# Turning the softmax reciprocals and the output gate on VectorE instead of TensorE

## The chip, the core and the metric

The kernel runs on one core of a Trainium2 chip. The metric is the device time of one execution in microseconds. Runs of the kernel before took 562.09 us as a median of three (561.46 to 562.93). A profile of one further execution stands beside them; its numbers are used below. TensorE is called PE in the rows, VectorE DVE, ScalarE ACT, GpSimd POOL, and SyncE, which issues most DMAs, SP.

## The reference

One encoder layer on 512 rows (8 by 64 tokens) of 1024 columns. All is float32.

```python
mod = silu(c) @ w_c + b_c                      # 3072 numbers
shift, scl, gate = split(mod, 3)
h = rms_norm(x, g_pre) * (1 + scl) + shift
xa, za, q, k, v, zb, ga, gb = split(h @ w_in, 8)
y_a = (rg_lru(conv(xa), forward) + rg_lru(conv(xa), backward)) * silu(za)
y_b = neighbourhood_attention(q, k, v, rpb) * silu(zb)   # 16 heads of 64; softmax over 8 x 16 neighbours
merged = sigmoid(ga) * (y_a @ w_pa) + sigmoid(gb) * (y_b @ w_pb)
out = rms_norm(x + gate * (merged @ w_o), g_final)
```

## The kernel before

Every product is taken in three passes of a one-pass float format: each float32 operand is split into a high and a low part (ACT casts the high part, DVE or POOL subtracts it), and `mm3` (L386) adds high x high, high x low and low x high in PSUM. `h` is kept with its 1024 columns on partitions as eight tiles of 128 x 512, and `proj` (L689) makes one tile of 128 columns of a projection from one 512 KB tile of weights: load, cast, subtraction, 24 matmuls.

The stages follow one another: start-up (`c`, norm, `h`) together with the projection for v to 60 us; attention, four groups of two pairs of heads, to about 262 us; the recurrent branch with the projection of y_b; the merge (`merge`, L1129) to about 490 us; and the output product with residual and final norm (`epi`, L1169).

The order of all instructions is written by a planner (`Plan`, L99). Each piece of work is an `op` with an engine, a cost, a rank, and the tiles that it reads and writes; the planner steps through its own time, and on each engine takes the piece with the lowest rank among those that can begin soonest. Tiles of 128 x 512 come from 36 slots (`T`), tiles of 128 x 1024 from 32 (`W`), PSUM from 8 banks with a limit for each class (`LIMITS`, L35). A load with `spare=n` is placed only when n more slots are free. `lock=True` keeps a DVE piece and POOL apart in the plan. `after` ties a piece to the begin of a projection, by its place in the list `main`. Each engine then executes its instructions in the written order, and SP's queue is in order too.

In the attention, `attend` (L797) takes the scores' softmax by blocks: DVE adds the bias and finds the minimum (L821), ACT takes the exponential and its sum into `sm`, TensorE turns the block (L835), ACT and DVE split it (L841, L843), and TensorE multiplies with v (L850). The sums `sm` of one pair of heads are 128 queries x 8 (4 blocks of queries by 2 heads). Their reciprocals are wanted along the free axis, one row for each head, spread over 64 partitions each. For that DVE takes the reciprocal (L877), TensorE turns 128 x 8 to 8 x 128 (L882, PSUM class `mi`), ACT copies it with a factor 0.5 (L883), SP writes it to a scratch in DRAM (L885), and two loads read it back spread over partitions (L888).

In the merge stage `gate_row` (L1084) computes the gate as a row: sixteen loads of 128 x 512 of w_c's last third, each multiplied with a column of silu(c) and added up over DVE (L1095, L1097), the sum over partitions by a matmul with ones in two passes (L1109, class `mi`), the bias added and halved (L1113, L1115). The two halves of the gate scale the rows of `w_o` before these are split (L1155). The shift and scale of the modulation are made otherwise, in the start-up: the transposed tile of w_c times the row of silu(c) (`silr`), summed along the free axis by one DVE instruction (L569).

In `epi` the last tile of rows has its right half in two pieces of 256 columns. For the last piece DVE squares and sums, ACT and DVE take the root and a Newton step, then DVE multiplies the right 512 columns by the row's factor and g_final (L1207) and SP writes them out, while ACT scales the left 512 columns (L1210) and writes them out from its own queue.

Of the kernel before, what the change touches and what calls it, by code (L numbers as in the profile page):

```python
# [331 lines left out]
@with_exitstack  # L332
def layer(ctx, tc, x, x_t, par, w_m, w_g, bc_gate, w_v, w_in, w_blk, rpb, amask, w_pa, w_pb, w_o, g_final, out):
    nc = tc.nc
# [60 lines left out]
    def const(name, shape, dt=F32):  # L395
        return pl.fixed(cp.tile(shape, dt, name=name))

    ident, onesc, onesr = const("ident", [P, P]), const("onesc", [P, P]), const("onesr", [P, P], F32R)
    prm, silc, msk, par_sb = const("prm", [P, 120]), const("silc", [P, KD]), const("msk", [P, 80]), const("par_sb", [120, P])
    tan8 = const("tan8", [8, P])  # L400
# [11 lines left out]
    pp0 = B("mi")  # L412
    op("PE", 0.25, lambda e: nc.tensor.transpose(pp0.ap[:, :120], par_sb.ap, ident.ap[:120, :120]), -20,
       r=[par_sb, ident], w=[pp0])
    op("DVE", 0.3, lambda e: nc.vector.tensor_copy(prm.ap, pp0.ap[:, :120]), -20, r=[pp0], w=[prm])
    pc = lambda a, b: prm.ap[:, a:b]
# [13 lines left out]
    for n in range(2):  # L430
        cb = B("hx")

        def f(e, n=n, cb=cb):
            for k in range(4):
                nc.tensor.matmul(cb.ap[:, k * P:(k + 1) * P], ident.ap[:120, 4 * n + k:4 * n + k + 1].to_broadcast([120, P]), par_sb.ap,
                                 start=True, stop=True)
# [96 lines left out]
    def modulate(k):  # L533

        for m, d in ((1, scs), (0, shs)):
# [4 lines left out]
            if k == 0:  # L540
# [18 lines left out]
                continue  # L559
            load(t, whole(t), w_m[2 * k + m], k - 5, 524288, spare=2, name=f"wc{k}{m}")  # L560
            if k == 1:
# [127 lines left out]
    def proj(w, rh, rl, lo="DVE"):  # L689
# [107 lines left out]
    def attend(pr, sps, z, nbt, pos, pos0):  # L797
# [3 lines left out]
        def half(bs):  # L801
# [70 lines left out]
        nz, oz = z  # L872
        sz, rc, rcb = T("sz"), C("rc", 8), B("mi")
        op("ACT", act(512), lambda e: nc.scalar.activation(sz.ap, oz.ap, AF.Tanh, scale=0.5), nz - 1.9, r=[oz], w=[sz], name="zt")
        op("DVE", dve(512), lambda e: nc.vector.scalar_tensor_tensor(sz.ap, sz.ap, 1.0, oz.ap, op0=ALU.add, op1=ALU.mult),
           nz - 1.9, r=[oz], rw=[sz], name="sz")
        op("DVE", 0.17, lambda e: nc.vector.reciprocal(rc.ap, sm.ap), pos - 0.3, r=[sm], w=[rc], name="rc")  # L877


        rct, rcx = T("rct"), T("rcx")  # L880
        scr = pl.fixed(dp.tile([8, P], F32, name=f"rscr{pr}"))
        op("PE", 0.15, lambda e: nc.tensor.transpose(rcb.ap[:8, :P], rc.ap, ident.ap), pos - 0.3, r=[rc, ident], w=[rcb], name="rcb")  # L882
        op("ACT", 0.3, lambda e: nc.scalar.activation(rct.ap[:8, :P], rcb.ap[:8, :P], AF.Copy, scale=0.5), pos - 0.3, r=[rcb], w=[rct],  # L883
           name="rct")
        op("SP", 0.5, lambda e: nc.sync.dma_start(scr.ap, rct.ap[:8, :P]), pos - 3, r=[rct], w=[scr], size=4096, late=SLACK, name="rcs")  # L885
        for h in range(2):
# [11 lines left out]
    def small(rank, after):  # L898
# [3 lines left out]
        op("ACT", 0.22, lambda e: nc.scalar.activation(lt[1].ap, lt[0].ap, AF.Exp, scale=-1.0), rank, r=[lt[0]], w=[lt[1]])  # L902
        op("DVE", 0.2, lambda e: nc.vector.tensor_scalar(silc.ap, pc(0, 8), 0.5, None, op0=ALU.mult), rank, r=[prm], w=[silc])

# [179 lines left out]
    def gate_row(pos, after):  # L1084
        op("ACT", 0.3, lambda e: nc.scalar.copy(onesr.ap, onesc.ap), pos, r=[onesc], w=[onesr], after=after)
        g = (T("g"), T("g"))
        for kk in range(KD):
            for n in range(2):
                wr = T("wr")
                load(wr, whole(wr), w_g[kk * P:(kk + 1) * P, n * 512:(n + 1) * 512], pos + 0.5 * kk, 262144,  # L1090
                     after=after, spare=12, name="wr")

                def f(e, kk=kk, n=n, wr=wr):
                    if kk == 0:
                        nc.vector.tensor_scalar(g[n].ap, wr.ap, silc.ap[:, 0:1], None, op0=ALU.mult)  # L1095
                    else:
                        nc.vector.scalar_tensor_tensor(g[n].ap, wr.ap, silc.ap[:, kk:kk + 1], g[n].ap, op0=ALU.mult, op1=ALU.add)  # L1097
                op("DVE", dve(512), f, pos + 3 + 0.5 * kk, r=[wr, silc], **({"rw": [g[n]]} if kk else {"w": [g[n]]}), lock=True,
                   name="grow")
        for n in range(2):  # L1100
            gh, gl = T("gh", F32R), T("gl", F32R)
            op("ACT", act(512), cast(whole(gh), whole(g[n])), pos + 8, r=[g[n]], w=[gh])
            op("DVE", dve(512), sub(whole(gl), whole(g[n]), whole(gh)), pos + 8, r=[g[n], gh], w=[gl], lock=True)
            o, bcg, gf = B("mi"), T("gate"), T("gfin")

            def f(e, gh=gh, gl=gl, o=o):
                mm(o.ap, onesr.ap, gh.ap, True, False)
                mm(o.ap, onesr.ap, gl.ap, False, True)
            op("PE", 0.46, f, pos + 8, r=[onesr, gh, gl], w=[o], name="grow")  # L1109
            load(bcg, whole(bcg), bc_gate[n * 512:(n + 1) * 512].partition_broadcast(P), pos + 7, 262144, after=after, spare=8)  # L1110

            def f(e, o=o, bcg=bcg):
                nc.vector.tensor_tensor(bcg.ap, o.ap, bcg.ap, op=ALU.add)  # L1113

                nc.vector.tensor_scalar(bcg.ap, bcg.ap, 0.5, None, op0=ALU.mult)  # L1115
            op("DVE", dve(512) + dve2(512), f, pos + 8.2, r=[o], rw=[bcg], lock=True, name="gate")
# [52 lines left out]
    def epi(t, c0, w, o, rank, last):  # L1169
# [150 lines left out]
```

## Time and profile before

| | |
|---|---|
| median of 3 runs | 562.09 us (561.46 to 562.93) |
| the profiled execution | 561.7 us, span 559.8 us |
| TensorE busy | 551.0 us, 98%, granted clock 0.999 |
| DVE, ACT, POOL busy | 391.2, 323.6, 101.9 us |
| chain that ended last | PE 88%, DMA 8%, SP queue 1%, DVE 1% |
| last matmul to the end of the span | 553.4 to 559.8 us |

The span runs from the first to the last instruction; the execution's time has 1.9 us more around it. Matmuls are pipelined: a single one shows its latency, and a piece of the chain of waits shows what a run of them took.

### The profile page before, as it was taken

To read this page: it belongs to the slowest core of one execution; us is meant where nothing else is said; L and a number is where in the kernel's file an instruction comes from. 1 tells how busy PE (TensorE), PEld (TensorE's weight loads), DVE (VectorE), ACT (ScalarE), POOL (GpSimd) and SP (SyncE) were. 2 spreads that over 40 slices of the span, in tenths; PEclk is the share of its full clock that TensorE was granted. 3 is DMA by queue.
4 is the path that set the end of the run, shared out by engine and by line. 5 is a ranking of instruction groups with operands and counts; after the bars stand their busy time and mean duration, and the time that the engine had idled before them with its cause. 6 is when DMAs were issued, how large, how long until landed. Compare 5 with 4: busy or idle time off the path is not lost.

```text
span 559.8 us, 7687 instructions
## 1 busy us (share of the span) xinstructions
PE 551.0 (98%) x2781; PEld 458.6 (82%) x2781; DVE 391.2 (70%) x696; ACT 323.6 (58%) x568; POOL 101.9 (18%) x95
## 2 busy tenths in 40 slices
PE   8999999999999999999999999999999999999995
PEld 8788888788888888887887888888788888888885
DVE  5999733684784876897569648866967897469523
ACT  6542623862763763787965984995698243223243
POOL 1103549555455440000000000000000000000220
PEclk9999999999999999999999999999999999999999
DMA  8993899346437434034332134032319462380002
GB/s 299 408 408 112 305 274 277 139 108 179 120 113 202 113 116 167 2 97 151 112 116 92 39 112 143 28 114 75 114 63 365 136 189 75 130 321 1 0 39 112
DMA packets 35580, 83.47 MB, mean 149 GB/s; under 512 B 3615, under 2 KB 10967, under 8 KB 35543
## 3 DMA queue, kind: packets, MB, share of 16 engines
q1 hardware_dynamic: 35264, 82.66, 44.6%
q8 instruction: 22, 0.36, 0.3%
q10 hardware_dynamic: 279, 0.32, 0.2%
q14 instruction: 15, 0.12, 0.1%
HBM read 76.65 MB, written 6.32 MB: 148 GB/s over the span
## 4 chain that ended last, share of the span: by engine, by line
PE 88%; DMA 8%; SPq 1%; DVE 1%; issue 0%; ACT 0%; POOL 0%; ACTq 0%; POOLq 0%
PE acc L384 72%; PE hx L384 8%; DMA wraw<-in_w_in_dram 3%; DMA vt<-vscr 3%; PE pv L384 3%; PE gt L384 2%; PE pt L835 2%; PE sp L384 2%; DMA wv<-in_w_v_dram 1%; DMA xT<-in_x_t_dram 1%; SPq L373 1%; SPq L678 1%; DVE va L675 0%; POOL vl L381 0%; PE mi L384 0%
## 5 line engine op out<-in xcount | busy, mean ns | idle before, releaser
L384 PE MATMUL acc<-hhl,whi 128*128 128x512 f32 x784 | 244.6, 393 | 0.0
L384 PEld LDWEIGHTS acc<-hhl,whi 128*128 128x128 f32 x784 | 143.9, 188 | 27.7
L384 PE MATMUL acc<-hhl,wlo 128*128 128x512 f32 x392 | 152.9, 390 | 0.0
L384 PEld LDWEIGHTS acc<-hhl,wlo 128*128 128x128 f32 x392 | 73.6, 188 | 15.6
L378 ACT CAST whi<-wraw 128x1024 fp32r<-128x1024 f32 x72 | 74.1, 1043 | 7.3 <-DMA wraw<-in_w_in_dram 6.6
L1186 POOL TENSOR_TENSOR yo<-yo,gfin 128x512 f32<-128x512 f32 x6 | 8.1, 1350 | 337.2 <-ACT xr L1183 337.2
L381 POOL TENSOR_TENSOR wlo<-wraw,whi 128x1024 fp32r<-128x1024 f32 x23 | 56.0, 2441 | 53.8 <-ACT whi L378 41.2
L381 DVE TENSOR_TENSOR wlo<-wraw,whi 128x1024 fp32r<-128x1024 f32 x49 | 59.2, 1220 | 9.3 <-ACT whi L378 9.1
L384 PE MATMUL acc<-woh,mhl 128*128 128x512 f32 (+1 forms) x144 | 40.4, 365 | 0.0
L384 PE MATMUL acc<-ybhl,whi 128*128 128x512 f32 x128 | 39.4, 389 | 0.0
L384 PE MATMUL acc<-yahl,whi 128*128 128x512 f32 x128 | 39.4, 389 | 0.0
L736 POOL TENSOR_TENSOR nb<-msk,braw 128x192 f32<-128x192 f32 (+1 forms) x48 | 30.7, 668 | 43.1 <-DMA braw<-in_rpb_dram 29.6
L828 ACT ACTIVATE p<-p,mn 128x192 f32<-128x192 f32 (+1 forms) x64 | 30.5, 477 | 5.8 <-DVE mn L821 5.7
L384 PE MATMUL hx<-vh,hhl 128*128 128x512 f32 x112 | 33.5, 389 | 0.0
L821 DVE CUSTOM_DVE_ANT_0 p<-sp,nb 128x192 f32<-128x192 f32 (+1 forms) x64 | 31.7, 607 | 0.9 <-PE sp L384 0.7
L1061 DVE SCALAR_TENSOR_TENSOR gm<-gm,acc 128x512 f32<-128x512 f32 x16 | 11.0, 687 | 28.6 <-PE acc L384 28.5
L384 PEld LDWEIGHTS acc<-woh,mhl 128*128 128x128 f32 x144 | 26.1, 189 | 4.4
L843 DVE TENSOR_TENSOR pp<-pt,pp 128x384 fp32r<-128x384 f32 (+1 forms) x32 | 19.8, 625 | 12.7 <-ACT pp L841 12.3
L384 PEld LDWEIGHTS acc<-yahl,whi 128*128 128x128 f32 x128 | 24.0, 188 | 5.0
L384 PEld LDWEIGHTS acc<-ybhl,whi 128*128 128x128 f32 x128 | 24.0, 188 | 5.0
L967 DVE SCALAR_TENSOR_TENSOR xc<-acc,prm,xc 128x511 f32<-128x511 f32 (+1 forms) x24 | 18.0, 749 | 12.3 <-ACT xc L960 11.7
L384 PE MATMUL acc<-wol,mhl 128*128 128x512 f32 (+1 forms) x72 | 26.3, 365 | 0.0
(202 smaller groups left out, 964.4 us busy)
## 6 DMA issues: line engine op xcount, KB each, us to landing
wraw<-in_w_in_dram SPq DMA_DIRECT2D x56, 512.0 KB
wc<-in_w_m_dram SPq DMA_DIRECT2D x14, 512.0 KB
vt<-vscr SPq DMA_DIRECT2D x24, 256.0 KB
vscr<-va SPq DMA_DIRECT2D x8, 512.0 KB
wraw<-in_w_pb_dram SPq DMA_DIRECT2D x8, 512.0 KB
wraw<-in_w_pa_dram SPq DMA_DIRECT2D x8, 512.0 KB
wr<-in_w_g_dram SPq DMA_DIRECT2D x16, 256.0 KB
wo<-in_w_o_dram SPq DMA_DIRECT2D x8, 512.0 KB
```

Of the source, the lines that this page charges most:

```text
L373: return op("SP", 0.45, lambda e: nc.sync.dma_start(dst(), src() if callable(src) else src), rank, r=r, w=[t], after=after, spare=spare, s ...
L378: return lambda e: nc.scalar.copy(o(), i()) if e == "ACT" else nc.vector.tensor_copy(o(), i())
L381: return lambda e: ENGINE[e].tensor_tensor(o(), a(), b().bitcast(F32), op=ALU.subtract)
L384: nc.tensor.matmul(o, a, b, start=first, stop=last)
L736: nc.gpsimd.tensor_tensor(o, mv, view, op=ALU.subtract)
L821: nc.vector.tensor_tensor_reduce(out=o, in0=v(spv(h, e)[:, :nk]), in1=v(nb[:, h, :nk]), scale=1.0, scalar=3e38, op0=ALU.add, op1=ALU.min, ...
L828: nc.scalar.activation(pv2(i), pv2(i), AF.Exp, bias=mn.ap[:, c:c + 1], scale=-1.0, accum_out=sm.ap[:, 2 * b + h:2 * b + h + 1])
L835: nc.tensor.transpose(ptp.ap[:, j * P:(j + 1) * P], pt_.ap[:, j * P:(j + 1) * P], ident.ap)
L843: op("DVE", dve(nt * P), lambda e_, ppv=ppv, pv4=pv4: nc.vector.tensor_tensor(ppv()[:, :, 1, :], pv4(), ppv()[:, :, 0, :].bitcast(F32), op ...
L967: nc.vector.scalar_tensor_tensor(a, b, wcol, a, op0=ALU.mult, op1=ALU.add)
L1061: op("DVE", dve(512), lambda e: nc.vector.scalar_tensor_tensor(t.ap, t.ap, 1.0, o.ap, op0=ALU.add, op1=ALU.mult), n - 1.9, r=[o], rw=[t], ...
L1186: op(("DVE", "POOL"), (dve(w), pool_(w)), lambda e: ENGINE[e].tensor_tensor(y(), y(), gfin[n].ap[:, gs], op=ALU.mult), rank + 0.1, r=[gfin ...
```

## The change

- `attend`: DVE doubles the 128 x 8 sums, takes the reciprocals into the first 8 columns of a fixed 128 x 32 tile (`rc0` or `rc1`, filled with ones once by POOL), and turns that tile in pieces of 32 by 32. SP writes the 128 x 32 result to a scratch of 32 x 128 in DRAM through the view `turned`, which puts piece b of 32 partitions at columns 32b: 128 runs of 32 numbers. The two loads that read rows back stay. The transpose on TensorE and the copy on ACT go.
- The gate is made as a column, like shift and scale: eight loads of 512 KB of the transposed w_c, at ranks 17 to 24, each times `silr` and summed by one DVE instruction, at ranks 20 to 27; then halved, turned in pieces of 32 by 32, and written to a scratch. `gate_row` now only loads the two halves from that scratch, spread over 128 partitions. The sixteen loads, the row's sums, its split and its four matmuls go, with the constants `onesr` and `silc`.
- The parameters' block has 128 rows in place of 120, as it takes in the gate's bias.
- `epi`: in the last tile the piece of columns 512 to 767 is multiplied by g_final as soon as it is squared. At the end DVE multiplies only columns 768 to 1023 by factor and g_final, then scales columns 448 to 767; SP writes columns 448 to 1023, and ACT scales and writes 0 to 447.

```diff
+GR = 17
...
-    op("PE", 0.25, lambda e: nc.tensor.transpose(pp0.ap[:, :120], par_sb.ap, ident.ap[:120, :120]), -20,
+    op("PE", 0.25, lambda e: nc.tensor.transpose(pp0.ap[:, :P], par_sb.ap, ident.ap), -20,
...
+    def turned(scr):
+        return bass.AP(scr.tensor, scr.offset, [[32, 4], [P, 32], [1, 32]])
...
+    rcs = [const(f"rc{i}", [P, 32]) for i in range(2)]
+    for t in rcs:
+        op("POOL", 0.1, lambda e, t=t: nc.gpsimd.memset(t.ap, 1.0), 8, w=[t], after=[main[6]])
...
-        sz, rc, rcb = T("sz"), C("rc", 8), B("mi")
+        sz, rc = T("sz"), rcs[pr % 2]
...
-        op("DVE", 0.17, lambda e: nc.vector.reciprocal(rc.ap, sm.ap), pos - 0.3, r=[sm], w=[rc], name="rc")
+        def recip(e):
+            nc.vector.tensor_scalar(rc.ap[:, :8], sm.ap, 2.0, None, op0=ALU.mult)
+            nc.vector.reciprocal(rc.ap[:, :8], rc.ap[:, :8])
+            nc.vector.transpose(rct.ap[:, :32], rc.ap)
...
-        scr = pl.fixed(dp.tile([8, P], F32, name=f"rscr{pr}"))
-        op("PE", 0.15, lambda e: nc.tensor.transpose(rcb.ap[:8, :P], rc.ap, ident.ap), pos - 0.3, r=[rc, ident], w=[rcb], name="rcb")
-        op("ACT", 0.3, lambda e: nc.scalar.activation(rct.ap[:8, :P], rcb.ap[:8, :P], AF.Copy, scale=0.5), pos - 0.3, r=[rcb], w=[rct],
-           name="rct")
-        op("SP", 0.5, lambda e: nc.sync.dma_start(scr.ap, rct.ap[:8, :P]), pos - 3, r=[rct], w=[scr], size=4096, late=SLACK, name="rcs")
+        scr = pl.fixed(dp.tile([32, P], F32, name=f"rscr{pr}"))
+        op("DVE", 0.5, recip, pos - 0.3, r=[sm], w=[rc, rct], name="rc")
+        op("SP", 0.5, lambda e: nc.sync.dma_start(turned(scr.ap), rct.ap[:, :32]), pos - 3, r=[rct], w=[scr], size=16384, late=SLACK, name="rcs")
...
+    gcol, gtur = const("gcol", [P, 32]), T("gtur")
+    gscr = pl.fixed(dp.tile([32, P], F32, name="gscr"))
+    op("POOL", 0.1, lambda e: nc.gpsimd.memset(gcol.ap, 0.0), 8, w=[gcol])
+    for k in range(KD):
+        t, r = W("wc"), gcol.part()
+        load(t, whole(t), w_m[3 * k + 2], GR + k, 524288, after=[main[GR + k - 2]], spare=6, name=f"wc{k}2")
+        op("DVE", dve(1024) + 0.08, lambda e, k=k, t=t: nc.vector.tensor_tensor_reduce(
+            out=t.ap, in0=t.ap, in1=silr.ap, scale=0.5, scalar=pc(120 + k, 121 + k), op0=ALU.mult, op1=ALU.add,
+            accum_out=gcol.ap[:, k:k + 1]), GR + 3 + k, r=[silr, prm], rw=[t], w=[r], lock=True, name="gate")
+    def turn(e):
+        nc.vector.tensor_scalar(gcol.ap[:, :8], gcol.ap[:, :8], 0.5, None, op0=ALU.mult)
+        nc.vector.transpose(gtur.ap[:, :32], gcol.ap)
+    op("DVE", 0.35, turn, GR + 12, rw=[gcol], w=[gtur], name="gturn")
+    op("SP", 0.5, lambda e: nc.sync.dma_start(turned(gscr.ap), gtur.ap[:, :32]), GR + 12, r=[gtur], w=[gscr], size=16384, late=SLACK, name="gscr")
...
     def gate_row(pos, after):
-        op("ACT", 0.3, lambda e: nc.scalar.copy(onesr.ap, onesc.ap), pos, r=[onesc], w=[onesr], after=after)
-        g = (T("g"), T("g"))
-        for kk in range(KD):
-            for n in range(2):
-                wr = T("wr")
-                load(wr, whole(wr), w_g[kk * P:(kk + 1) * P, n * 512:(n + 1) * 512], pos + 0.5 * kk, 262144,
-                     after=after, spare=12, name="wr")
...
         for n in range(2):
...
-            op("PE", 0.46, f, pos + 8, r=[onesr, gh, gl], w=[o], name="grow")
-            load(bcg, whole(bcg), bc_gate[n * 512:(n + 1) * 512].partition_broadcast(P), pos + 7, 262144, after=after, spare=8)
...
+            bcg, gf = T("gate"), T("gfin")
+            load(bcg, whole(bcg), bass.AP(gscr.ap.tensor, gscr.ap.offset + n * 512, [[0, P], [1, 512]]), pos + 7, 262144, r=[gscr],
+                 after=after, spare=8)
...
-            if t < NT - 1 or n == 0:
+            if t < NT - 1 or c0 + w < D:
                 op(("DVE", "POOL"), (dve(w), pool_(w)), lambda e: ENGINE[e].tensor_tensor(y(), y(), gfin[n].ap[:, gs], op=ALU.mult),
...
-            z, zz = (lambda: yo[t].ap[:, 512:]), (lambda: yo[t].ap[:, :512])
-            op("DVE", dve(512), lambda e: nc.vector.scalar_tensor_tensor(z(), z(), rs.ap, gfin[1].ap, op0=ALU.mult, op1=ALU.mult),
-               rank, r=[rs, gfin[1]], rw=[yo[t]], lock=True)
-            op("SP", 0.45, lambda e: nc.sync.dma_start(out[rows, 512:], z()), rank, r=[yo[t]], size=262144)
-            op("ACT", act(512, 1) + 0.5, lambda e: (nc.scalar.activation(zz(), zz(), AF.Copy, scale=rs.ap),
-               nc.scalar.dma_start(out[rows, :512], zz())), rank, r=[rs], rw=[yo[t]])
+            z, zz, c1 = (lambda: yo[t].ap[:, 448:]), (lambda: yo[t].ap[:, :448]), c0 - 448
+            def scale(e):
+                nc.vector.scalar_tensor_tensor(y(), y(), rs.ap, gfin[n].ap[:, gs], op0=ALU.mult, op1=ALU.mult)
+                nc.vector.tensor_scalar(z()[:, :c1], z()[:, :c1], rs.ap, None, op0=ALU.mult)
+            op("DVE", dve(w) + dve2(c1), scale, rank, r=[rs, gfin[n]], rw=[yo[t]], lock=True)
+            op("SP", 0.45, lambda e: nc.sync.dma_start(out[rows, 448:], z()), rank, r=[yo[t]], size=294912)
+            op("ACT", act(448, 1) + 0.5, lambda e: (nc.scalar.activation(zz(), zz(), AF.Copy, scale=rs.ap),
+               nc.scalar.dma_start(out[rows, :448], zz())), rank, r=[rs], rw=[yo[t]])
```

## Rows read from the trace of the kernel before

**Rows 1.** The page: busy us of each engine, share of span, instructions.

```profile
PE 551.0 (98%) x2781; PEld 458.6 (82%) x2781; DVE 391.2 (70%) x696; ACT 323.6 (58%) x568; POOL 101.9 (18%) x95
```

**Rows 2.** TensorE's waits: who, for whom, us in total, times, longest.

```profile
PE hx L502 <- POOL epsc L450: 1.5, 1, 1.5
PE pv L384 <- DVE pp L843: 0.4, 1, 0.4
```

**Rows 3.** Chain of waits: start us, us, what; the pieces named mi and the last.

```profile
108.60 0.11 PE mi L882
...
250.43 0.11 PE mi L882
...
469.85 0.46 PE mi L384 x2
...
471.02 0.46 PE mi L384 x2
471.47 81.95 PE acc L384 x384
```

**Rows 4.** Instructions on tile rc: count, ns min/median/max, first and last start us.

```profile
L877 DVE RECIPROCAL rc<-sm x8: 202/203/218, 107.4 to 249.3; 128x8 f32<-128x8 f32 x8
...
L882 PE MATMUL mi<-ident,rc x8: 270/271/273, 108.4 to 250.3; 128*8 128x128 f32 x8
```

**Rows 5.** Waits of SP's queue.

```profile
SPq L885 <- ACT rct L883: 65.2, 8, 21.3
```

**Rows 6.** Timeline of SP's queue: start us, us, what; the last pair of heads.

```profile
250.87 0.30 SPq L885 DMA_DIRECT2D rscr<-rct  x1
252.23 1.24 SPq L373 DMA_DIRECT2D rcx<-rscr  x2
```

**Rows 7.** Instructions of line 569, the reductions of the modulation, ns min/median/max.

```profile
L569 DVE CUSTOM_DVE_ANT_0 wc<-wc,silr,prm x6: 1275/1276/1280, 20.7 to 49.7; 128x1024 f32<-128x1024 f32 x6
...
L569 DVE CUSTOM_DVE_ANT_0 wc<-wc,silr,mods x6: 1337/1340/1702, 23.7 to 48.1; 128x1024 f32<-128x1024 f32 x6
L569 DVE DVE_READ_ACCUMULATOR2_ANT sc<- x6: 78/82/84, 25.0 to 49.7; 128x1 f32 x6
```

**Rows 8.** Stretches of the attention: us, busy us by engine, clock, DMA share, GB/s.

```profile
101.23:124.25 23.02, 23.02 (x129) 19.52 (x130) 18.71 (x43) 17.60 (x49) 12.24 (x11) 1.00 0.33 101
124.25:137.19 12.94, 12.94 (x59) 10.42 (x58) 6.22 (x10) 4.23 (x7) 7.77 (x6) 1.00 0.82 221
...
167.51:180.46 12.95, 12.95 (x60) 10.43 (x58) 6.22 (x10) 4.23 (x7) 7.78 (x6) 1.00 0.78 221
...
223.71:255.10 31.39, 31.39 (x201) 26.66 (x200) 28.71 (x68) 22.98 (x59) 0.00 (x0) 1.00 0.18 53
```

**Rows 9.** Timeline, attention: start us, us, engine, what; DVE, TensorE and POOL.

```profile
108.57 0.69 DVE L843 TENSOR_TENSOR pp<-pt,pp 128x512 fp32r<-128x512 f32 x1
...
110.75 0.63 PE L384 MATMUL pv<-pp,vt 128*128 128x256 f32 x4
...
164.84 2.40 POOL L381 TENSOR_TENSOR wlo<-wraw,whi 128x1024 fp32r<-128x1024 f32 x1 [2.99 <-ACT whi L378]
...
165.49 2.31 DVE L381 TENSOR_TENSOR ybhl<-sz,ybhl 128x512 fp32r<-128x512 f32 x1
...
176.29 0.68 DVE L381 TENSOR_TENSOR ybhl<-sz,ybhl 128x512 fp32r<-128x512 f32 x1
```

**Rows 10.** Timeline of the tail, behind the last matmul.

```profile
553.44 0.42 DVE L1175 TENSOR_TENSOR yo<-acc,xr 128x256 f32<-128x256 f32 x1 [0.89 <-PE acc L384]
...
555.35 0.72 ACT L1210 ACTIVATE yo<-yo,rs 128x512 f32<-128x512 f32 x1 [0.68 <-DVE rs L1203]
555.35 0.75 DVE L1207 SCALAR_TENSOR_TENSOR yo<-yo,rs,gfin 128x512 f32<-128x512 f32 x1
...
556.12 0.33 SPq L1209 DMA_DIRECT2D out_dram<-yo  x1
```

**Rows 11.** Instructions of line 1095, a scaling of 512 columns by a pointer.

```profile
L1095 DVE TENSOR_SCALAR g<-wr,silc x2: 479/479/479, 423.4 to 423.8; 128x512 f32<-128x512 f32 x2
```

More of the change, by code (lines that the diff above doesn't have):

```diff
@@ L332, in layer @@
 @with_exitstack
-def layer(ctx, tc, x, x_t, par, w_m, w_g, bc_gate, w_v, w_in, w_blk, rpb, amask, w_pa, w_pb, w_o, g_final, out):
+def layer(ctx, tc, x, x_t, par, w_m, w_v, w_in, w_blk, rpb, amask, w_pa, w_pb, w_o, g_final, out):
     nc = tc.nc
@@ L396, in const @@
         return pl.fixed(cp.tile(shape, dt, name=name))
-    ident, onesc, onesr = const("ident", [P, P]), const("onesc", [P, P]), const("onesr", [P, P], F32R)
-    prm, silc, msk, par_sb = const("prm", [P, 120]), const("silc", [P, KD]), const("msk", [P, 80]), const("par_sb", [120, P])
+    ident, onesc = const("ident", [P, P]), const("onesc", [P, P])
+    prm, msk, par_sb = const("prm", [P, P]), const("msk", [P, 80]), const("par_sb", [P, P])
     tan8 = const("tan8", [8, P])
@@ L412, in layer @@
     pp0 = B("mi")
-    op("PE", 0.25, lambda e: nc.tensor.transpose(pp0.ap[:, :120], par_sb.ap, ident.ap[:120, :120]), -20,
+    op("PE", 0.25, lambda e: nc.tensor.transpose(pp0.ap[:, :P], par_sb.ap, ident.ap), -20,
        r=[par_sb, ident], w=[pp0])
-    op("DVE", 0.3, lambda e: nc.vector.tensor_copy(prm.ap, pp0.ap[:, :120]), -20, r=[pp0], w=[prm])
+    op("DVE", 0.3, lambda e: nc.vector.tensor_copy(prm.ap, pp0.ap[:, :P]), -20, r=[pp0], w=[prm])
     pc = lambda a, b: prm.ap[:, a:b]
@@ L434, in f @@
             for k in range(4):
-                nc.tensor.matmul(cb.ap[:, k * P:(k + 1) * P], ident.ap[:120, 4 * n + k:4 * n + k + 1].to_broadcast([120, P]), par_sb.ap,
+                nc.tensor.matmul(cb.ap[:, k * P:(k + 1) * P], ident.ap[:, 4 * n + k:4 * n + k + 1].to_broadcast([P, P]), par_sb.ap,
                                  start=True, stop=True)
@@ L559, in modulate @@
                 continue
-            load(t, whole(t), w_m[2 * k + m], k - 5, 524288, spare=2, name=f"wc{k}{m}")
+            load(t, whole(t), w_m[3 * k + m], k - 5, 524288, spare=2, name=f"wc{k}{m}")
             if k == 1:
@@ L902, in small @@
         op("ACT", 0.22, lambda e: nc.scalar.activation(lt[1].ap, lt[0].ap, AF.Exp, scale=-1.0), rank, r=[lt[0]], w=[lt[1]])
-        op("DVE", 0.2, lambda e: nc.vector.tensor_scalar(silc.ap, pc(0, 8), 0.5, None, op0=ALU.mult), rank, r=[prm], w=[silc])
         ab, ee, ss, s_2, pol = (t.ap for t in lt)
@@ L1084, in gate_row @@
     def gate_row(pos, after):
-        op("ACT", 0.3, lambda e: nc.scalar.copy(onesr.ap, onesc.ap), pos, r=[onesc], w=[onesr], after=after)
-        g = (T("g"), T("g"))
-        for kk in range(KD):
-            for n in range(2):
-                wr = T("wr")
-                load(wr, whole(wr), w_g[kk * P:(kk + 1) * P, n * 512:(n + 1) * 512], pos + 0.5 * kk, 262144,
-                     after=after, spare=12, name="wr")
[L1093 to L1099, printed above, removed]
-        for n in range(2):
[L1101 to L1108, printed above, removed]
-            op("PE", 0.46, f, pos + 8, r=[onesr, gh, gl], w=[o], name="grow")
-            load(bcg, whole(bcg), bc_gate[n * 512:(n + 1) * 512].partition_broadcast(P), pos + 7, 262144, after=after, spare=8)
[L1112 to L1116, printed above, removed]
+        for n in range(2):
+            bcg, gf = T("gate"), T("gfin")
+            load(bcg, whole(bcg), bass.AP(gscr.ap.tensor, gscr.ap.offset + n * 512, [[0, P], [1, 512]]), pos + 7, 262144, r=[gscr],
+                 after=after, spare=8)
             gate.append(bcg)
@@ L1281 @@
     w_in = a["w_in"].reshape(D, 8 * D)
-    mod = a["w_c"].reshape(D, 3, KD, P)[:, :2].transpose(2, 1, 3, 0).copy()
+    mod = a["w_c"].reshape(D, 3, KD, P).transpose(2, 1, 3, 0).copy()
     mod[0, 1] = tiles(a["w_c"].reshape(D, 3 * D)[:, D:D + P])[0]
@@ L1287 @@
         f("c"), f("g_pre"), f("b_c")[:2 * D], f("conv_w"), f("conv_b"),
-        f("b_r_f"), swap(f("b_i_f")), f("b_r_b"), swap(f("b_i_b")), f("lam_f"), f("lam_b"),
-    ]).reshape(120, P)
+        f("b_r_f"), swap(f("b_i_f")), f("b_r_b"), swap(f("b_i_b")), f("lam_f"), f("lam_b"), f("b_c")[2 * D:],
+    ]).reshape(P, P)
     pad = np.zeros((1, PAD), np.float32)
@@ L1295 @@
         "par": par,
-        "w_m": mod.reshape(2 * KD, P, D),
-        "w_g": a["w_c"].reshape(D, 3 * D)[:, 2 * D:],
-        "bc_gate": f("b_c")[2 * D:].copy(),
+        "w_m": mod.reshape(3 * KD, P, D),
         "w_v": w_in[:, 4 * D:5 * D].reshape(KD, P, D),
```

## The prediction

> **What bounds the kernel now.** I read the engines' busy time first, then TensorE's waits, then the chain of waits, and last the stretches that the change touches. TensorE is busy for 98% of the span and DVE for 70% [rows 1]. TensorE's longest wait is 1.5 us in the start-up, and behind the start-up there is one in the whole run, 0.4 us, for the DVE subtraction that makes the low part of the probabilities [rows 2]. In the stretches from 101.23 us on TensorE is busy for every microsecond [rows 8], and the chain of waits ends with 82 us of its matmuls in one piece, up to 553.4 us [rows 3]. So a microsecond of TensorE work that goes is a microsecond of the time, and work that goes from DVE, ACT or POOL is worth nothing, unless it made TensorE wait. The reader should see that two kinds of small TensorE work stand in that chain under the name `mi`: the transposes of the softmax reciprocals and the broadcast of the gate row.
>
> **The change, part by part.**
>
> *TensorE work removed.* The eight transposes of the reciprocals (L882) each stand in the chain with 0.11 us, the first at 108.60 and the last at 250.43 [rows 3]: 8 x 0.11 = 0.88 us. (An instruction's own 0.27 us [rows 4] is its latency through the pipelined array; what it costs TensorE is the piece of the chain.) The gate row's two pairs of matmuls with the ones stand there with 0.46 us each [rows 3]: 0.92 us. Together 1.80 us, and nothing is put on TensorE for it. The wider first transpose (128 columns of parameters for 120) and the 128 rows for 120 in the broadcast of c lie in the start-up, which waits for x and w_v; I take 0, and not over 0.05 us either way.
>
> *Reciprocal, now on DVE alone.* Before: one reciprocal of 0.20 us [rows 4], then TensorE, ACT, SP. After: a multiplication, the reciprocal and a transpose of 128x32 on DVE. A transpose on DVE is not in the trace. The nearest rows from below and above are that 128x8 instruction of 0.20 us and the 128x256 addition of 0.42 us [rows 4, 10]; it has 32 columns, so I take 0.20. With 0.2 for the multiplication that is +0.4 us of DVE per pair of heads (0.4 to 0.65), 3.2 us in all. It lies in the attention's dense stretches, where DVE is busy 18.71 of 23.02 us and, in the last, 28.71 of 31.39 [rows 8]. Two pairs fall in each stretch, so +0.8 us there: it still fits (2.7 us free in the tightest). Price 0 as long as it stands in no subtraction's way; if all of it did, 3.2 us.
>
> *The way through DRAM.* SP's queue stood 65.2 us in all, in 8 waits, for `rct` from ACT [rows 5]. The scratch writes now come sooner by TensorE's and ACT's turn, 0.27 us for TensorE's alone [rows 4]. But each is 16 KB in 128 pieces of 128 B where it was 4 KB in 8 rows of 512 B, and the two reads of the row wait for it at the head of SP's queue, with a load of weights behind them. Before, the last write was issued at 250.87 and the reads at 252.23, 1.36 us later [rows 6]. The price of a 128 B piece is not in these rows: from below it is nothing more, from above I let the wait double, +1.36 us. I take +0.5 us of SP time, half of it paid for by the sooner start. On the time: 0, and nothing below, because TensorE never waited for a row of reciprocals. With the cover gone it would be up to 8 x 1.36 = 10.9 us of SP, not of TensorE, as weights are loaded some five projections ahead.
>
> *The gate column.* Sixteen loads of 256 KB and the DVE work on them in the merge stage go; eight loads of 512 KB and eight reductions over 1024 columns come into the attention. The same reduction takes 1.28 us (1.70 at most), its accumulator's read 0.08 [rows 7]: 8 x 1.36 = 10.9 us of DVE. In the two stretches in which TensorE does projections alone, 124.25 to 137.19 and 167.51 to 180.46, DVE is busy 6.22 of 12.94 us [rows 8]: 6.7 us free in each, 13.4 together, enough for all eight. The loads need 4.2 MB; those stretches already move 221 GB/s at a DMA share of 0.8, but the dense ones between move 101 at a third [rows 8], so there is room. Held-up loads would only push the gate later, and it is not needed before `wo` is scaled. Price: 0, if the order keeps the reductions out of the dense stretches; the other end is the slower rival below.
>
> One rule speaks against this part. POOL's weight subtractions take 2.40 us, and beside one of them DVE's 128x512 subtraction for `ybhl` took 2.31 us, where it takes 0.68 alone [rows 9]. The Trainium skill, SBUF — State Buffer, section "Who interferes with whom", says that a DVE instruction with two SBUF inputs and a GpSimd instruction that reads SBUF exclude each other, and that the later one is blocked until the first has finished. The trace agrees (2.31 for 0.68). By that rule the reductions, which also read two SBUF tensors, can each grow by 1.63 us, and what that would do is the slower rival.
>
> *The merge stage.* DVE and ACT get time back there. No wait of TensorE's is behind them [rows 2], so this is worth 0; the next work late there is TensorE's own.
>
> *The tail.* After the last matmul the chain is DVE and ACT to 556.1 us, then two output DMAs. ACT scales 448 columns for 512: 0.72 us [rows 10] less 0.05. DVE's one instruction of 512 columns, 0.75 us [rows 10], becomes two. The first is the same on 256 columns: 0.75 less 0.26 (0.68 for 512 [rows 9] against 0.42 for 256 [rows 10]) = 0.49. The second is a scaling of 320 columns by a pointer: 0.48 for 512 [rows 11], by its length down to 0.30 and with none of it saved 0.48; I take 0.38. Two in a row overlap by 0.08 (the pair of rows 11 begins 0.4 us apart, with 0.48 each): 0.79 in all, +0.04 us on SP's branch and -0.05 on ACT's, and SP's piece grows from 256 to 288 KB. The added multiplication by g_final of 256 columns lies beside the last matmuls; if the wait for it showed, it would be at most the 0.42 us of rows 10. I take 0 for the tail, -0.05 to +0.25.
>
> **The sum.** The profiled execution took 561.7 us, 1.9 of it outside its span of 559.8. Span after: 559.8 - 0.88 - 0.92 + 0 = 558.0; time 559.9. That execution lies 0.39 below the median of the runs, 562.09, so I predict 560.3 as a median.
>
> **The rivals.**
>
> *Slower: DVE keeps TensorE waiting in the attention.* The written order changes everywhere behind the first reduction, and one that falls into a dense stretch stands in front of a subtraction that feeds the product with v. How much is there to spare? The subtraction that begins at 108.57 ends at 109.26, and its product begins at 110.75 [rows 9]: 1.5 us. A plain reduction of 1.36 us fits under that; one that meets POOL takes 1.36 + 1.63 = 3.0 us and costs 1.5. Two such pass the 1.80 us gained: from there on the change is a loss. Three of the eight cost 4.5 us: 562.1 - 1.8 + 4.5 = 564.8. For it: DVE is over 80% busy there, and the one wait of TensorE's is of this kind [rows 2, 8]. Against it: the order is planned with 1.3 us for each reduction and with POOL and DVE kept apart, the plan before left 0.4 us of waits, and there are lulls enough. Chance 0.13.
>
> *No change that can be measured.* One or two smaller waits of this kind, or the same wait as before made longer (it follows a load of weights that lands late, and the vector of c now keeps one of the wide buffers for longer): 0.8 to 1.8 us lost, 560.9 to 562.1. For: every order planned anew places its waits anew. Against: as above. Chance 0.20.
>
> *More than the sum.* The wait of 0.44 us goes as well, and the sooner reciprocal and the free PSUM bank let the plan close small gaps: 562.1 - 1.8 - 0.5 = 559.8. Chance 0.10.
>
> *It doesn't take the matmuls' time out.* That would be so if the transposes filled time in which TensorE waited anyway: 562.1. Against: before and behind them the chain is TensorE's, without a gap [rows 3]. Chance 0.03.
>
> **How the numbers follow.** The forecast has the chance left over, 0.54. Runs of one kernel here lie between 561.46 and 562.93, and about 0.3% (1.7 us) is what a measurement of it can tell from no change. My 1.8 us lies just beyond that: of the forecast's 0.54 I put 0.38 under 560.4 us and 0.16 above. Faster is 0.38 + 0.10 + 0.02 of the second rival = 0.50; same 0.16 + 0.18 + 0.03 = 0.37; slower 0.13. The range runs from the third case less what runs differ by, 559.2, to one lost wait of 1.5 us and as much spread above, 562.7.
>
> **What would show it right or wrong.** Right: no `mi` piece in the chain behind the start-up, TensorE's busy time down by about 1.8 us, and its waits after 101 us under 0.5 us. The reductions stand in the stretches of pure projections, or a little before, with 1.3 us each. From the last matmul to the end it is 6.4 us as now. Wrong: TensorE waits for DVE's `pp` or for a score's minimum between 100 and 262 us, with a reduction of over 2 us ahead of it on DVE (the slower rival); waits for weights behind the reads of `rscr` (the scatter); or a tail that differs by over 0.2 us.

## The result, and the profile after

Predicted was 560.3 us, faster. Measured: 564.52 us as a median of 21 runs (560.95 to 566.99), beside 562.12 for the kernel before in as many runs (560.92 to 564.85). The ratio is 1.0035, with an interval of 1.0022 to 1.0049: slower, and outside the predicted range. The profiled execution took 565.04 us, its span is 563.2.

The page of the kernel after, its busy time (answers to [rows 1]):

```profile
PE 551.7 (98%) x2769; PEld 458.3 (81%) x2769; DVE 392.0 (70%) x708; ACT 320.7 (57%) x557; POOL 103.2 (18%) x99
```

Twelve matmul instructions have gone, but TensorE is busy for 0.7 us longer, where 1.8 less was forecast: it did less work and did some of it more slowly. Its waits (engine, what it waited for; us, times, longest; answers to [rows 2]):

```profile
PE pv L385 <- DVE pp L851: 3.3, 2, 2.9
PE hx L503 <- POOL epsc L451: 1.5, 1, 1.5
```

The wait for `pp`, 0.4 us before, is now 2.9 us and has a second beside it. The chain of waits, for [rows 3]:

```profile
93.24 8.46 DMA wraw<-in_w_in_dram
...
101.78 0.07 ACT whi L379
...
102.73 0.48 ACT pp L849
103.23 0.57 DVE pp L851
103.85 0.74 PE pv L385 x4
...
106.93 1.29 PE acc L385 x3
...
112.54 1.44 DVE rc L887
...
403.82 152.89 PE acc L385 x696
```

No `mi` piece is left, and the last 153 us are matmuls in one piece: what was to be removed is removed. But the chain now runs through a load of weights that was issued at 93.24 and took 8.46 us, the cast of these weights on ACT, the copy and the subtraction that make `pp`, and then TensorE. The same on the timeline (start, us; in brackets how long the engine had been idle, and for what):

```profile
101.78 1.04 ACT L379 CAST whi<-wraw 128x1024 fp32r<-128x1024 f32 x1 [5.61 <-DMA wraw<-in_w_in_dram]
...
103.23 0.56 DVE L851 TENSOR_TENSOR pp<-pt,pp 128x384 fp32r<-128x384 f32 x1 [4.96 <-ACT pp L849]
103.85 0.74 PE L385 MATMUL pv<-pp,vt 128*128 128x256 f32 x4 [2.89 <-DVE pp L851]
...
116.01 0.74 PE L385 MATMUL pv<-pp,vt 128*128 128x256 f32 x4 [0.44 <-DVE pp L851]
```

ACT executes in order, so the cast that waits 5.61 us for its load holds the copy of the probabilities behind it; DVE stands 4.96 us for that copy, and TensorE 2.89 us for DVE. And then the stretches (columns as in [rows 8]; the second and third are those behind that wait):

```profile
101.00:104.00 3.00, 0.15 (x1) 0.15 (x2) 0.77 (x2) 2.22 (x7) 1.10 (x1) 1.00 1.03 331
104.00:108.00 4.00, 4.00 (x17) 3.31 (x18) 2.81 (x10) 2.95 (x10) 1.29 (x1) 0.62 0.62 197
108.00:112.00 4.00, 4.00 (x22) 3.43 (x21) 3.30 (x7) 3.44 (x9) 0.46 (x1) 0.96 0.04 16
...
128.81:141.75 12.94, 12.94 (x60) 10.45 (x58) 9.38 (x14) 4.40 (x7) 4.49 (x2) 1.00 0.98 236
```

The same 4 us in the kernel before:

```profile
104.00:108.00 4.00, 4.00 (x24) 3.37 (x23) 3.53 (x10) 3.77 (x11) 0.55 (x1) 1.00 0.01 3
```

Having stood idle for most of the first stretch, TensorE then gets a granted clock of 0.62 over 4 us, a mean between its two levels (1.2 and 2.4 GHz); in the kernel before the same 4 us have 1.00 and 24 matmul records in place of 17. At 0.62 these 4.00 us hold 2.5 us of work: 1.5 us are lost, and counted as busy; the next 4 us, at 0.96, lose another 0.2. So of the span's +3.4 us 2.8 are accounted for: 2.5 us of longer wait (2.89 for 0.44), 1.7 us of clock and 0.44 us of second wait, less the 1.8 us removed. Of the other 0.6, 0.14 lie ahead of the attention (its first scores begin at 93.21 for 93.07) and 0.1 in the tail; some 0.4 I can't place. Nearly all of the loss lies ahead of 141 us: the group of scores that began at 137.19 [rows 8] begins at 141.75, 4.56 us later, and the last matmul ends only 3.30 us later (556.72 for 553.42).

The rest of the rows. The reciprocal's three instructions on tile `rc`, and the gate's reductions (counts, ns min/median/max; [rows 4, 7]):

```profile
L887 DVE TENSOR_SCALAR rc<-sm x8: 161/172/1424, 112.5 to 253.9; 128x8 f32<-128x8 f32 x8
L888 DVE RECIPROCAL rc<-rc x8: 202/203/204, 114.0 to 254.1; 128x8 f32<-128x8 f32 x8
L889 DVE STREAM_TRANSPOSE rct<-rc x8: 211/211/215, 114.2 to 254.4; 128x32 f32<-128x32 f32 x8
...
L959 DVE CUSTOM_DVE_ANT_0 wc<-wc,silr,prm x8: 1276/1280/2511, 109.5 to 171.8; 128x1024 f32<-128x1024 f32 x8
```

SP's queue at the last pair of heads, the scatter and the reads behind it ([rows 6]), and the tail ([rows 10]):

```profile
254.60 0.56 SPq L895 DMA_DIRECT2D rscr<-rct  x1
256.69 1.24 SPq L374 DMA_DIRECT2D rcx<-rscr  x2
...
558.64 0.67 ACT L1212 ACTIVATE yo<-yo,rs 128x448 f32<-128x448 f32 x1 [0.68 <-DVE rs L1201]
558.64 0.48 DVE L1208 SCALAR_TENSOR_TENSOR yo<-yo,rs,gfin 128x256 f32<-128x256 f32 x1
559.05 0.38 DVE L1209 TENSOR_SCALAR yo<-yo,rs 128x320 f32<-128x320 f32 x1
...
559.45 0.33 SPq L1211 DMA_DIRECT2D out_dram<-yo  x1
```

The issue of a scatter takes 0.56 us for 0.30, and the reads come 2.09 us behind it for 1.36. The tail is 6.48 us for 6.38.

### The profile page after: what moved, and what is told of

Same layout as the page of the kernel before. It is cut to its first block, busy times and chain, and to the rows that moved or that the text cites. A ratio compares the mean times of both kernels' runs of the same rounds, so it can differ in the third digit from the quotient of the medians.

```text
span 563.2 us, 7661 instructions
## 1 busy us (share of the span) xinstructions
PE 551.7 (98%) x2769; PEld 458.3 (81%) x2769; DVE 392.0 (70%) x708; ACT 320.7 (57%) x557; POOL 103.2 (18%) x99
## 4 chain that ended last, share of the span: by engine, by line
PE 91%; DMA 5%; DVE 2%; ACT 0%; issue 0%; SPq 0%; DVEq 0%; ACTq 0%
PE acc L385 76%; PE hx L385 6%; DMA wv<-in_w_v_dram 3%; PE pv L385 3%; PE gt L385 2%; PE pt L843 2%; PE sp L385 2%; DMA wraw<-in_w_in_dram 2%; DMA xT<-in_x_t_dram 1%; SPq L374 0%; DVE rc L887 0%; DVE vl L382 0%; DVE wc L959 0%; DVE pp L851 0%; ACT vh L379 0%
## 5 line engine op out<-in xcount | busy, mean ns | idle before, releaser
L1184 POOL TENSOR_TENSOR yo<-yo,gfin 128x512 f32<-128x512 f32 (+1 forms) x7 | 8.8, 1263 | 338.9 <-ACT xr L1181 335.0
```

## The experiments

Three theories stood after the result, and the letters are those of the expectations. **A**: the bytes of the gate column's loads, which begin at 96 us, delay the weight for which ACT waits. **B**: the work added on DVE, reductions and doublings, stands ahead of `pp`. **C**: the late weight is no part of the change. It stands in SP's queue behind eight loads of v and lands when it lands, in both kernels. For C speaks the queue, here of the kernel before and then of the kernel after:

```profile
81.96 9.12 SPq L373 DMA_DIRECT2D vt<-vscr  x8
91.57 2.55 SPq L373 DMA_DIRECT2D wraw<-in_w_in_dram  x3
```

```profile
84.05 9.06 SPq L374 DMA_DIRECT2D vt<-vscr  x8
93.24 2.23 SPq L374 DMA_DIRECT2D wraw<-in_w_in_dram  x3
96.07 0.33 SPq L374 DMA_DIRECT2D wc<-in_w_m_dram  x1
```

The order is the same up to the first `wc`: eight loads of v hold SP for 9 us, and three weights come behind them. The scores of the second group of heads, which needs this v, begin only at 137 us. And what the late weight holds up, on ACT of the kernel before:

```profile
99.16 1.05 ACT L378 CAST whi<-wraw 128x1024 fp32r<-128x1024 f32 x1 [3.14 <-DMA wraw<-in_w_in_dram]
100.11 0.48 ACT L841 CAST pp<-pt 128x384 fp32r<-128x384 f32 x1
```

The runs were made on three chips, each time beside the kernel before (medians of 563.03, 563.09 and 561.58 us): the first four kernels on one, the next four on a second, the last four on a third. The ratio takes in all runs and is not that of the two medians.

**One part at a time.** The kernel before with the reciprocals alone:

```diff
+            nc.vector.tensor_scalar(rc.ap[:, :8], sm.ap, 2.0, None, op0=ALU.mult)
+            nc.vector.reciprocal(rc.ap[:, :8], rc.ap[:, :8])
+            nc.vector.transpose(rct.ap[:, :32], rc.ap)
...
-        op("PE", 0.15, lambda e: nc.tensor.transpose(rcb.ap[:8, :P], rc.ap, ident.ap), pos - 0.3, r=[rc, ident], w=[rcb], name="rcb")
```

> The kernel before with the first part of the change alone: reciprocals turned by DVE and scattered through DRAM; the gate stays a row as before, the tail too. Theory A (the gate's first loads, issued at 96.07 and 100.67 us, lengthen a stretch of TensorE idling at 101 us that ends on late weights, and the half clock behind it costs as much again): 562.1 - 0.88 = 561.2, with a wait of 0.4 us or so at 101 us. Theory B (DVE's order: the reciprocal's doubling took 1.42 us beside POOL and put the subtraction for the product with v off): 0.4 to 1 us lost for several of the pairs, 562 to 565. Theory C (the stretch at 101 us waits for weights by chance, in any kernel with this order of loads): like A.

Measured: 561.55 us (12 runs), ratio 0.9979 (0.9959 to 0.9999). And the change without it, gate and tail alone:

```diff
-            nc.vector.tensor_scalar(rc.ap[:, :8], sm.ap, 2.0, None, op0=ALU.mult)
-            nc.vector.transpose(rct.ap[:, :32], rc.ap)
...
+        op("PE", 0.15, lambda e: nc.tensor.transpose(rcb.ap[:8, :P], rc.ap, ident.ap), pos - 0.3, r=[rc, ident], w=[rcb], name="rcb")
```

> The change without its first part: the reciprocals by TensorE and ACT as before, the gate as a column in the attention, the new tail. Theory A: 562.1 - 0.92 + 4.2 = 565.4, the wait at 101 to 104 us as in the changed kernel, granted clock under 1 behind it. Theory B: 561.2 if the reciprocals alone are to blame; if the reductions are, 563 to 565 with TensorE waits for DVE behind them. Theory C: 561.2 in the runs in which the weights are in time.

Measured: 562.64 us (12 runs), ratio 1.0006 (0.9982 to 1.0029). The wait for `pp` and the stretch behind it, first of the reciprocals alone:

```profile
PE pv L384 <- DVE pp L851: 1.7, 1, 1.7
```

```profile
104.00:108.00 4.00, 4.00 (x23) 3.46 (x23) 3.45 (x9) 3.88 (x11) 0.00 (x0) 1.00 0.04 17
```

And of the gate and the tail alone:

```profile
PE pv L385 <- DVE pp L848: 2.7, 2, 1.9
```

```profile
104.00:108.00 4.00, 4.00 (x16) 3.21 (x15) 2.41 (x7) 2.81 (x8) 0.04 (x1) 0.58 0.48 170
```

The wait is there with either part, also without any load of the gate. The times don't size the terms of 0.88 and 0.92 us: the intervals reach from 0.1 to 2.3 us gained for the reciprocals and from 1.0 gained to 1.6 lost for the gate and tail, and the kernel before had far more runs in its upper half here than these two (table below). After a wait of 1.7 us the clock stayed at 1.00, after 1.9 it was 0.58. The second wait of the gate and tail alone is theory B's:

```profile
119.65 3.27 DVE L954 CUSTOM_DVE_ANT_0 wc<-wc,silr,prm 128x1024 f32<-128x1024 f32 x1
...
125.41 0.74 PE L385 MATMUL pv<-pp,vt 128*128 128x256 f32 x4 [0.82 <-DVE pp L848]
```

A reduction that began at 119.65, while POOL was at a weight subtraction (119.46 to 121.84), took 3.27 us for 1.28, and the product behind it waited 0.82 us for `pp`.

**The bytes of the gate's loads.** The written order of the change, but loads of 8 columns of 1024; the reductions read `silr` twice and keep their length:

```diff
-        load(t, whole(t), w_m[3 * k + 2], GR + k, ...)
+        load(t, lambda t=t: t.ap[:, :8], w_m[3 * k + 2, :, :8], GR + k, ...)
...
-            out=t.ap, in0=t.ap, in1=silr.ap, ...
+            out=t.ap, in0=silr.ap, in1=silr.ap, ...
```

> The changed kernel in the same order on every engine, but each of the gate's eight loads moves 8 of 1024 columns, and the reductions read the row of silu(c) twice in their place, so the gate comes out otherwise. DVE's work is the same. Theory A: the loss goes, 562.1 - 1.8 + 0.5 = 560.8, with under 1 us of wait at 101 us. Theory B: as the changed kernel, 564.5. Theory C: as the changed kernel too, since the needed weights were issued before the first of these loads.

Measured: 561.49 us (12 runs), ratio 0.9989 (0.9967 to 1.001). The time seems to speak for A, though the changed kernel itself did not run on this chip; the profile (the wait, and the stretch behind it) does not:

```profile
PE pv L385 <- DVE pp L851: 3.1, 2, 2.7
```

```profile
104.00:108.00 4.00, 4.00 (x17) 3.37 (x16) 2.32 (x8) 2.55 (x10) 0.82 (x1) 0.58 0.16 57
```

Without the bytes TensorE waited 2.7 us all the same. Then the gate's loads six ranks later:

```diff
-GR = 17
+GR = 23
```

> The changed kernel with the gate's loads and reductions six ranks later (GR = 23): the first load is tied to the begin of the 22nd piece of the main list in place of the 16th, some 45 us later, in a stretch that moves 106 GB/s. Theory A: 560.5 to 561. Theory B: the reductions meet dense stretches there too, 563.5 to 564.5. Theory C: 564, as the order of loads up to 95 us is the same.

Measured: 561.76 us (12 runs), ratio 0.9992 (0.997 to 1.0014), one run over 563 us; in its profile the longest wait is 0.5 us.

**The change again, and the late weight.** On the second chip the changed kernel was repeated as it is.

> The changed kernel itself, beside the next three on one chip. Theory C (TensorE idles at 101 us because the weights of the next projections stand in SP's queue behind eight loads of v that are not needed for another 35 us; by how much differs from run to run, in the kernel before too; idling that lasts about 2 us or more is followed by some 4 us at half clock): 562 to 565, and the wait in the profile can be anything from 0.5 to 3 us. Theory A (the gate's loads at 96 us): 564 to 565 with a wait of 2 us or more.

Measured: 561.81 us (560.28 to 567.32, 12 runs), ratio 0.9996 (0.9971 to 1.002): even with before. Its profiled run is one of the long ones and shows the same picture, a wait of 2.6 us and then a clock of 0.62. With it ran the kernel before with one edit, the second group's loads of v one rank later, so that a weight goes ahead of them:

```diff
-                load(a, ..., src, 8 + 6 * g - 1.5 + 0.1 * (b > 0), n * 2048,
+                load(a, ..., src, 8 + 6 * g - 1.5 + VO * (g == 1) + 0.1 * (b > 0), n * 2048,      # VO = 1.0
```

> The kernel before with one rank changed: the second set of eight loads of v (for the second group of heads) one rank later, so that one load of weights passes ahead of it in SP's queue, issued at about 82 in place of 91.6 us. Nothing else differs in SP's order. Theory C: no wait at 101 us, no half clock in any run, 560.5 to 561.5, and less spread than before. Theory A: as before, 562 to 563, the wait of 0.4 us stays.

Measured: 561.18 us, ratio 0.997 (0.9956 to 0.9984), and all 12 runs between 560.65 and 561.54, where before had 561.07 to 565.68. Its queue and its cast:

```profile
82.14 0.66 SPq L374 DMA_DIRECT2D wraw<-in_w_in_dram  x1
83.25 9.78 SPq L374 DMA_DIRECT2D vt<-vscr  x8
...
96.47 1.03 ACT L379 CAST whi<-wraw 128x1024 fp32r<-128x1024 f32 x1
```

The weight is issued at 82.14 in place of 91.57, and its cast no longer waits for a DMA. That is 0.3% for no part of the change, on a chip on which before had 17 of 32 runs over 563 us, and the spread of 4.6 us has shrunk to 0.9: most of what the runs of the kernel before differ by there goes with this one load. The same edit on the changed kernel:

```diff
+VO = 1.0        # in the kernel after
```

> The changed kernel with the same one rank changed. Theory C: the wait at 101 us goes; what is left is the sum of the prediction less the 0.44 us behind the reciprocal, 1.0 to 1.8 us under the kernel before with the same edit (559.5 to 560.5). Theory A: the gate's loads still stand in the full stretch, so it stays 1 us or more over the kernel before with this edit.

Measured: 560.62 us (12 runs, one over 563), ratio 0.9962 (0.9941 to 0.9983). TensorE still waits once for `pp`, 0.6 us, and the chain of waits and the timeline show for what:

```profile
96.99 9.46 DMA wc<-in_w_m_dram
...
106.48 1.28 DVE L960 CUSTOM_DVE_ANT_0 wc<-wc,silr,prm 128x1024 f32<-128x1024 f32 x1 [1.26 <-DMA wc<-in_w_m_dram]
...
112.07 0.73 PE L386 MATMUL pv<-pp,vt 128*128 128x256 f32 x4 [0.55 <-DVE pp L852]
```

Here it is the gate's own load that is late: the first reduction stands on DVE until it has landed, 9.46 us after its issue, and `pp` comes behind it. Then the edit together with the gate's loads at rank 23 and no doubling (the factor 0.5 goes into the two instructions that make y_b's parts):

```diff
+VO = 1.0
-GR = 17
+GR = 23
...
-            nc.vector.tensor_scalar(rc.ap[:, :8], sm.ap, 2.0, None, op0=ALU.mult)
-            nc.vector.reciprocal(rc.ap[:, :8], rc.ap[:, :8])
+            nc.vector.reciprocal(rc.ap[:, :8], sm.ap)
...
+        op("ACT", act(512), lambda e: nc.scalar.activation(ybh[pr].ap, sz.ap, AF.Copy, scale=0.5), ...
+        op("DVE", dve(512), lambda e: nc.vector.scalar_tensor_tensor(ybl[pr].ap, sz.ap, 0.5, ybh[pr].ap.bitcast(F32), op0=ALU.mult, op1=ALU.subtract), ...
```

> The changed kernel with v later, the gate's loads six ranks later, and the doubling in front of the reciprocals taken out (the factor 0.5 goes into the split of the product, at no instruction). If the wait at 101 us, the loads and the doubling beside POOL (1.42 us for 0.17) are the whole loss: 559 to 560, TensorE's waits after the start-up under 0.3 us. If DVE's order as such costs TensorE: waits of 0.4 us or more at the reductions' places, 560.5 or more.

Measured: 559.52 us (559.06 to 560.85, 9 runs), ratio 0.9941 (0.9922 to 0.9961), faster than both kernels. Against before with the same later loads of v that is 561.18 - 559.52 = 1.66 us: nearly all of the 1.80 us of TensorE's work.

**What is left open by that.** On the third chip the changed kernel ran a third time.

> The changed kernel a third time, beside the next one on the same chip. Late weight (the wait exists in both kernels and its length is luck): runs in two heaps, about 560.5 to 562 and 563 to 567 us, and a ratio to the kernel before between 0.998 and 1.002. If the change itself shifts the odds: most runs over 563 us and a ratio of 1.002 to 1.005, as when it was first measured.

Measured: 563.37 us (12 runs, 7 over 563), ratio 1.0016 (0.9995 to 1.0037). Beside it once more the one with the small loads.

> The written order of the changed kernel, the eight loads of the gate column with 8 of 1024 columns each (the gate comes out otherwise). Against the changed kernel on the same chip. If the bytes of the gate's loads lengthen the wait for the late weight: 0.3 to 0.5% faster than the changed kernel, fewer than 3 of 12 runs over 563 us. If they don't: equal within 0.2%, and as many runs in the upper heap.

Measured: 564.53 us (12 runs, 9 over 563), ratio 1.0037 (1.0015 to 1.0058). With the bytes taken away it was no faster than the change on the same chip. Theory A, for the wait at 101 us, falls by the time too, and its first, better-looking figure was the chip or luck. Its profiled run is a short one, with a wait of 0.6 us where the same kernel had 2.7 on the first chip: the length of this wait belongs to the run and not to the kernel. Next the change with later loads of v and without doubling, the gate's loads left at rank 17:

```diff
+VO = 1.0
...
-            nc.vector.tensor_scalar(rc.ap[:, :8], sm.ap, 2.0, None, op0=ALU.mult)
```

> The changed kernel with the second group's v loads one rank later, and without the doubling of the sums (the factor 0.5 moved into the two instructions that make y_b's parts); the gate loads stay at rank 17. Before with the same later v loads took 561.18, and 1.80 us of matmuls are out: if the doubling in front of pp was the rest of the loss, 559.4 to 559.8, as the version that also loads the gate at rank 23. If the loads at rank 17 were, 560.3 to 560.8, as the changed kernel with later v loads took.

Measured: 560.53 us, ratio 1.0002 (0.9978 to 1.0026). Neither expectation describes it. The median lies in the second's range, but no run does: seven runs took 559.53 to 560.87, with a mean clock of 0.997 to 0.999, and five 563.36 to 564.67, with 0.993 or 0.994. The profiled run is one of the seven and has no wait for `pp`. And the version that took 559.52 us again, which differs from this one by `GR = 23` alone:

> The version with later v loads, no doubling and the gate's loads at rank 23, again on another chip. Expected as before, 559.3 to 559.8 and a spread under 2 us: a ratio to the kernel before of 0.993 to 0.996. If its first measurement was luck of one chip: 560.5 and more.

Measured: 559.54 us (559.24 to 560.35, 10 runs), ratio 0.9959 (0.9944 to 0.9974). Its busy time, and all of TensorE's waits that the view lists:

```profile
PE 549.4 (99%) x2769; PEld 457.3 (82%) x2769; DVE 389.3 (70%) x700; ACT 320.9 (58%) x557; POOL 103.0 (18%) x99
```

```profile
PE hx L504 <- POOL epsc L452: 1.5, 1, 1.5
```

TensorE is busy for 1.6 us less than before [rows 1], and it waits for nothing behind the start-up. In this version the promised time is there, on two chips.

How many runs of each kernel took over 563 us (the mark is mine; it lies between the two heaps of the kernel with rank 17):

| kernel | first measurement | chip 1 | chip 2 | chip 3 |
|---|---|---|---|---|
| before | 4 of 21 | 19 of 35 | 17 of 32 | 3 of 33 |
| the change | 18 of 21 | | 5 of 12 | 7 of 12 |
| the change, small loads | | 3 of 12 | | 9 of 12 |
| reciprocals alone; gate and tail alone; gate at rank 23 | | 2, 4, 1 of 12 | | |
| before, loads of v later | | | 0 of 12 | |
| the change, loads of v later | | | 1 of 12 | |
| the same, doubling out | | | | 5 of 12 |
| the same, doubling out, gate at rank 23 | | | 0 of 9 | 0 of 10 |

## Why the prediction was wrong, point by point

- **TensorE's work removed, 1.80 us: right.** No `mi` piece is left, and where the waits are gone the time is 1.66 us shorter than before with the same loads of v, and TensorE's busy time 1.6.
- **The step that failed: the gate column, "Price: 0", and with it a sum that carried the one wait behind the start-up over at the 0.4 us of [rows 2].** That wait hangs on a load that stands behind eight others in SP's queue, and the cast of it stands ahead of `pp` on ACT. It was 0.4, 0.5, 0.6, 1.7, 1.9, 2.3, 2.6, 2.7 or 2.9 us long in the profiles of kernels in which the loads of v were not moved, the change or not. I read one execution's 0.4 as a property of the kernel; most of the spread of its runs, which stood beside it, goes with this wait. For the scatter I had reckoned that held-up loads cost SP and not TensorE, as weights are loaded some five projections ahead. TensorE did not wait for the weight: counted in order, the one issued at 91.57 in the kernel before serves the projection that begins at 119.61. It waited for the copy that makes `pp`, which stands on ACT behind this weight's cast. I named the case (the same wait made longer, as it follows a load of weights that lands late), but priced it at 0.8 to 1.8 us, without the clock: the profiled run lost 2.5 us by the wait and 1.7 by the clock. That the slower rival's 564.8 us lies next to the measured 564.52 is luck: its reductions beside POOL are not what this run lost its time by.
- **The gate column's place.** I had all eight reductions in the stretches of pure projections. Five stand in dense stretches, at 109.5, 120.8, 143.8, 151.3 and 158.8, and three in the lulls (DVE busy 9.38 us in the first for the 6.22 of [rows 8]). Beside POOL a reduction can grow by more than my 1.63 us: the 3.27 us of the gate and tail alone are 2.0 more than 1.28, and cost 0.82 us where the slower rival had 1.5. That its loads fit because a stretch's average share has room was no argument: what counts is what waits at that moment, and once DVE stood 1.26 us for such a load. The bytes don't lengthen the wait at 101 us, as the small loads show. With the loads of v later and the doubling out, rank 17 leaves five long runs of 12 and rank 23 none of 10 on the same chip: so the part has a price at rank 17 there, 1.0 us by the medians (560.53 and 559.54).
- **The reciprocal on DVE, +0.4 us for each pair: right in size, wrong once in place.** The transpose was put at 0.20 and took 0.211. But one doubling took 1.42 us for 0.17. It began at 112.54 beside a subtraction of POOL's:

```profile
111.54 2.39 POOL L382 TENSOR_TENSOR wlo<-wraw,whi 128x1024 fp32r<-128x1024 f32 x1 [6.25 <-ACT whi L379]
...
112.54 1.42 DVE L887 TENSOR_SCALAR rc<-sm 128x8 f32<-128x8 f32 x1
```

  POOL's ends at 113.93 and the doubling at 113.96. The Trainium skill (SBUF — State Buffer, "Who interferes with whom") says that a `tensor_scalar` can take both of DVE's port pairs, of which GpSimd shares one, and that whichever comes later is blocked for the whole of the other's instruction. The trace agrees (1.42 us, to POOL's end). I had weighed that section for the reductions and not for the smallest instruction of all. Behind that doubling and the reduction at 109.53 the product of 116.01 waited 0.44 us, the slower rival's mechanism at a tenth of its price.
- **The scatter, +0.5 us of SP: right in size.** +0.26 us by the issue and up to 0.73 to the reads at the last pair, and TensorE never waited for it.
- **The tail, 0: right.** 6.48 us for 6.38; the two DVE instructions took 0.48 and 0.38 us as worked out, ACT's 0.67.

What stays open: why the changed kernel lost in the first measurement and on the third chip and was even on the second. The kernel before moves as much from chip to chip (3 of 33 to 19 of 35), so part of it is where the late weight lands on a chip; but on the third chip before had 3 long runs of 33 and the change 7 of 12, so there the change does shift the odds. What of it, the reductions, the doublings or merely a new order, has not been separated; and where the five long runs of the version with rank 17 lose their time was not seen, as none of them was profiled. A gate load that holds DVE, as with later loads of v alone, is a candidate that no run has tested. The mean clock of the five (0.994 for 0.998) can't be turned into time lost: the profile of the kernel after has 0.993, and 2.1 of the 3.9 us that this lacks lie behind its last matmul (a clock of 0.67 over 6.5 us), where they cost nothing.

## What to carry to other kernels

A wait of one profiled execution is a sample: if it ends with a DMA, see what stands ahead of that DMA in its queue and compare the spread of the runs, before it is carried over as a constant. Ask of each load when it is needed: here eight loads that came too early, in front of one that was due, cost as much on one chip as the change could gain (1.9 us by the medians), and one rank of difference was worth 0.3%. Ask as well what is written behind the first instruction that uses a load: it waits too, though it needs nothing of it. And a wait of TensorE's may have to be paid for twice, by the wait and by the clock after it; both belong in a rival's price.

## What the runs showed of the hardware that was not expected

After TensorE had been idle for 1.9, 2.3, 2.6, 2.7 and 2.9 us its granted clock over the following 4 us was 0.58, 0.59, 0.62, 0.58 and 0.62; after 1.7, 0.6 and 0.5 us it was 1.00. In these 4 us that is 1.5 to 1.7 us lost, beside the wait itself.

A DVE instruction of 128 by 8 numbers took 0.17 us alone and 1.42 us beside a POOL subtraction. A transpose of 128x32 in pieces of 32 by 32 took 0.211 us in all eight cases.

The same kernel's runs differ by chip: before had a median of 563.03, 563.09 and 561.58 us on three. With one load put ahead of eight others the spread of 4.6 us on the second fell to 0.9.
